# Where the last transposes of a SwiGLU's shares stand in the DMA queue, and where their first quarter is added

## The chip, the cores and the metric

The kernel runs on one core of a Trainium2 chip. The metric is the device time of one execution in microseconds (us), the median of several runs. Times inside the profile are us from the start of its span. The engines are named as the profile names them: PE (TensorE), DVE (VectorE), ACT (ScalarE), POOL (GpSimd) and SP (SyncE), whose queue here only issues DMAs.

## The reference

Two layers, on x of 512 tokens by 1024 features, in float32:

```
for l in range(2):
    x = x + 0.5 * swiglu(rms_norm(x, g1[l]), wg1[l], wu1[l], wd1[l])      # width 2816
    h = rms_norm(x, gm[l])
    z = h @ w_in[l]                                                       # 2304 columns
    attn = sliding_window_attention(q, k, v from z, sink)                 # 8 heads of 64, window 128
    conv = b_gate * causal_conv3(c_gate * h_conv)
    x = x + concat(attn, conv) @ w_out[l]
    x = x + 0.5 * swiglu(rms_norm(x, g2[l]), wg2[l], wu2[l], wd2[l])
return rms_norm(x, final)

swiglu(h, wg, wu, wd) = (silu(h @ wg) * (h @ wu)) @ wd
```

## The kernel before

x is kept with features on the partitions: eight tiles `xs[c]` of 128 features by 512 tokens, two to an `xpair`. Each product is made of three float32r matmuls, high by high, low by high and high by low. So each weight tile that has been loaded (`raw`) is split: ACT casts it to `wh` (line 226), DVE subtracts that from it into `wl` (line 226 too), 128 x 1024 elements at a time. `order` is the list of weight tiles in the order of use; `take_split` hands out the next one and splits those up to two further on (`SPLIT_AHEAD`); `need_split` in turn calls `need_raw`, which puts the loads of tiles up to four further on (`LOAD_AHEAD`) into SP's queue, at that place of the program. There are 8 `raw` buffers and 3 each for `wh` and `wl`.

A SwiGLU is a list of stages. The three inner ones (first and second of layer 0, first of layer 1) have the list `INNER`: a plain stage "p" and its down projection "d" with one block; five "w" stages (two blocks of the width each, by a scheme of seven products); two groups of shares "s", which are the down projections of four blocks each, by seven products; and a last "d", the down projection of blocks 9 and 10.

The shares make their result the other way round, with tokens on the partitions, in `Apart`. It is kept as four quarters (o, t): o is the half of the features, t the half of the tokens. Three go back to x through the DMA: `Apart.send` has ACT lay the 16-bit halves of the words apart (`lay_apart`, line 141, two copies a quarter) and SP issue two DMA transposes (line 898); `Apart.back` has ACT join the halves (line 911, two copies of 128 x 1024 a quarter) and DVE add them to x (line 915, two additions). The fourth, (0, 1), goes through PE (eight transposes, line 921) and two additions by DVE (line 926). In the second group of shares `SENT_AT` sends (0, 0) after step 3, (1, 1) after step 4 and (1, 0) after step 5; after step 6, the last, `between` calls `back(1, 1)`.

Then comes the last "d". It has four weight tiles, d0 to d3, each for two of the eight feature tiles, and makes them in the order c = 4, 5, 6, 7, 0, 1, 2, 3, twelve matmuls each. After each, DVE adds the result to `xs[c]` (line 1250). After c = 4 `BACK_AT` calls `back(0, 0)` and `back(0, 1)`, after c = 5 `back(1, 0)`. The next norm's `take` (ACT line 458 makes `xh`, DVE line 459 makes `xl`) and `square` (ACT line 467, DVE line 468) follow for each c as `FINAL_AT` says. The next stage's first matmuls take `xh` and `xl` in the same order of c, and after its first group and two more steps PE needs the sum of squares (line 523).

The weights of the next stage are loaded by the same rule of four ahead. It puts two loads into SP's queue before the transposes of (1, 1), and two more before those of (1, 0). ACT, DVE and SP each run their instructions in the order in which they are queued.

This passage, the end of the second group of shares and the last "d", occurs three times. Its places are called here J1 (first SwiGLU of layer 0, PE starts the "d" at 313.55 us), J2 (second SwiGLU of layer 0, at 796.12) and J3 (first SwiGLU of layer 1, at 1118.50). After J1 and J3 comes the mixing with its weights `w_in`, after J2 the next SwiGLU with `wg` and `wu`.

Of the kernel before, what the change touches and what calls it, by code (L numbers as in the profile page):

```python
# [49 lines left out]


SENT_AT = {3: (0, 0), 4: (1, 1), 5: (1, 0)}
BACK_AT = {4: ((0, 0), (0, 1)), 5: ((1, 0),)}
FINAL_AT = {4: (), 5: (4, 5)}
STREAM_BACK_AT = {9: 0, 11: 1, 16: 2, 18: 3}
SCORES_AT = (5, 6, 7, 8, 9, 10, 12, 13)
# [10 lines left out]
LOAD_AHEAD = 4  # L67
# [8 lines left out]
def trunk_kernel(  # L76
# [23 lines left out]
    nc = tc.nc  # L100
# [92 lines left out]
    units = []  # L193
    order = []
    raw_of, split_of = {}, {}
    roomy = set()
    state = {"raw": 0, "split": 0, "group": 0, "late": None}

    def add_unit(*unit):
        units.append(unit)  # L200
# [10 lines left out]
    def need_raw(u):  # L211

        while state["raw"] <= min(u, len(units) - 1):
            n = state["raw"]
            _, _, kc, _, wide = units[n][0]
            name, shape = f"raw_{n}", (P, kc, wide)
            r = form(name, F32, shape) if n in roomy else stock(name, shape=shape)
            if n >= OPEN:
                load(r, n, 0, kc)
            for more in units[n][1:]:  # L220
                nc.gpsimd.dma_start(out=r, in_=rows_of(*more), accum_op=ALU.add)  # L221
            raw_of[n] = r
            state["raw"] += 1
# [10 lines left out]
    def need_split(g):  # L234
        while state["split"] <= min(g, len(order) - 1):
            n = state["split"]
            u, what = order[n]
            far = what == "far"
            if what in (None, "far"):
                need_raw(u if far else u + LOAD_AHEAD)  # L240
                raw = raw_of.pop(u)
            elif isinstance(what, tuple) and what[0] == "end":

                _, what, h = what
                at = {"a11": 2, "s2": 2, "s3": 3, "s1": 3, "a12": 4, "a22": 5, "s4": 5}[what]
                need_raw(u + 3 * at + h + LOAD_AHEAD)
                raws = {name: u + 3 * i + h for i, name in enumerate(END_LOADS)}
                if what == "s2":
                    with tc.issue_after(state["rest"]):
                        nc.vector.tensor_add(raw_of[raws["a11"]], raw_of[raws["a11"]], raw_of[raws["s1"]])  # L250
                raw = raw_of[raws["a11" if what in ("s2", "s4") else what]]
            elif isinstance(what, tuple):

                what, h, how = what
                far = how == "far"
                last = {"a11": 0, "a12": 4, "s2": 2, "s3": 6, "s1": 2, "a22": 8, "s4": 4}[what]
                need_raw(u + h if far else u + max(last, 4) + h + LOAD_AHEAD)
                a11, s1, a12, s3, a22 = (raw_of.get(u + 2 * i + h) for i in range(5))
                if what == "s2":

                    late = state["late"] if h else None
                    if not state["late"] and how == "share":
                        late = state["rest"]
                    with tc.issue_after(late) if late else nullcontext():
                        nc.vector.tensor_add(a11, a11, s1)  # L265
                raw = {"a11": a11, "a12": a12, "s2": a11, "s3": s3, "s1": s1, "a22": a22, "s4": a12}[what]
            shape = list(raw.shape)
            hi = wpool.tile(shape, F32R, tag="wh", bufs=3, name=f"wh_{n}")
            lo = wpool.tile(shape, F32R, tag="wl", bufs=3, name=f"wl_{n}")
            if far:  # L270
                sent = split_far(hi, lo, raw)
            else:
                state["cast"], state["rest"] = (i.ins for i in split(hi, lo, raw))
            if isinstance(order[n][1], tuple) and order[n][1][0] == "end":
                if what == "a12":
                    nc.gpsimd.dma_start(out=raw_of[raws["a11"]], in_=raw, accum_op=ALU.add)
                if what in ("s3", "s1", "a12", "a22"):
                    del raw_of[raws[what]]
                if what == "s4":
                    del raw_of[raws["a11"]]  # L280
            elif isinstance(order[n][1], tuple):
                if what == "s3" and how == "share":
                    nc.gpsimd.dma_start(out=a12, in_=a11, accum_op=ALU.add)
                elif what == "s3":
                    nc.vector.tensor_add(a12, a12, a11)
                done = {"s3": (0, 3), "s1": (1,), "a22": (4,), "s4": (2,)}.get(what, ())
                for i in done:
                    del raw_of[u + 2 * i + h]
            split_of[n] = (hi, lo)
            state["split"] += 1  # L290
            if far:

                with tc.issue_after(sent.ins):
                    need_raw(u + LOAD_AHEAD + (4 + h if isinstance(order[n][1], tuple) else 0))
# [63 lines left out]
    def plan():  # L358
# [19 lines left out]
        def ffn(wg, wu, wd, stages, near=False):  # L378
            for what, b in stages:
                how = "far" if b == (0,) and not near else None  # L380
                if what == "p":
                    plain(wg, wu, b)
                if what == "w":
                    seven(
                        lambda o, j, h: ((wg, wu)[o], KC // 2 * j + 2 * h, 2, 2 * b * P, S),
                        lambda what, h: "far" if (b, what, h) == (1, "a11", 0) else None,
                    )
                if what == "s":
                    seven(
                        lambda o, j, h: (wd, 2 * b + KC // 2 * j + 2 * h, 2, o * S, S),  # L390
                        lambda what, h: "share",
                    )
                if what == "d":
                    cols(wd, 2 * b[0], 2 * len(b), KC, how, len(b) == 2)
                if what == "e":
                    u = len(units)
                    roomy.update(range(u, u + 3))
                    for form_ in END_LOADS:
                        ojs = {"s1": ((1, 0), (1, 1)), "s3": ((1, 0), (0, 0))}
                        for i in range(3):  # L400
                            add_unit(
                                *(
                                    (wd, 2 * b + (KC + 2 * j if i == 2 else KC // 2 * j + 2 * i), 2, o * S, S)
                                    for o, j in ojs.get(form_, ((0, int(form_ == "a12")) if form_ != "a22" else (1, 1),))
                                )
                            )
                    order.extend((u, ("end", what, i)) for what in END_FORMS for i in range(3))
# [470 lines left out]
    class Apart:  # L878
# [14 lines left out]
        def send(self, o, t):  # L893

            to = self.sent[o, t] = g8(f"turned_{self.name}_{o}_{t}", U16, (P, 2, NT, H))
            for u in range(2):
                halves = lay_apart(self.y[2 * t + u, o], f"{self.name}_{o}_{2 * t + u}")
                nc.sync.dma_start_transpose(
                    to.rearrange("p a c s -> p (a c) s")[:, :, u * P : (u + 1) * P],
                    halves.rearrange("p a n -> p (a n)"),  # L900
                )

        def back(self, o, t):

# [27 lines left out]
    def ffn(norm, stages, after=None, late=None):  # L932
# [248 lines left out]
        for i, (what, b) in enumerate(stages):  # L1181
# [22 lines left out]
            elif what == "e":  # L1204
                end.last(ends, kept)
                return
            elif what == "s" and b == sevens[0]:
                then = shared(sevens[1])
                share(
                    ops,  # L1210
                    0.5,
                    joined(ahead(then, {3: ("b11",), 4: ("b21",), 5: ("t2",), 6: ("t3",)})),
                    apart,
                    still=kept,
                )
            elif what == "s":

                def between(step):
                    if step == 1:
                        crossing[0].rejoin(1)  # L1220
                    if step in (4, 5):
                        with tc.issue_after(state["rest"]):
                            crossing[0].parts(step - 4)
                    if step in SENT_AT:
                        apart.send(*SENT_AT[step])
                    if step == 6:
                        apart.back(1, 1)

                share(then, 0.5, between, apart, behind=(1, 2, 3), on=kept)
# [10 lines left out]
            for c, acc in down(rhs, b == (0,), final):  # L1240
# [11 lines left out]
                    )  # L1252
                flush()
                if final:
                    for quarter in BACK_AT.get(c, ()):
                        apart.back(*quarter)
                    for k in FINAL_AT.get(c, (c,)):
# [478 lines left out]
```

## Time and profile before

| | us |
|---|---|
| median of 3 runs (lowest, highest) | 1630.61 (1630.34, 1632.09) |
| the profiled execution's own time | 1632.9 |
| its span, first to last instruction | 1631.1 |
| PE busy | 1616.7 |
| DVE busy | 1368.8 |
| ACT busy | 1178.1 |
| POOL busy | 223.6 |

The granted TensorE clock was 0.999 of full speed. Rows of a timeline give the start, the length, the engine, the line, the operation, what it writes and reads, how many such instructions the row merges, and in square brackets the time for which the engine stood idle before it and what ended that. A row of waits gives who waited for whom, the sum in us, the number of times and the longest. Matmul ends are modelled: a 128 x 512 matmul is shown as 0.39 long, and when nothing holds PE up the next one starts 0.227 after it.

### The profile page before, as it was taken

The numbers are of one execution on the slowest core, as the hardware profiler recorded it, in microseconds if no ns is written. First come the engines' busy times: TensorE is split into PE (matmuls) and PEld (weight loads), VectorE is DVE, ScalarE is ACT, GpSimd is POOL, SyncE is SP. The second block draws the span as 40 slices with busy tenths as digits, with TensorE's granted clock in tenths as the row PEclk, the third lists the DMA queues.
The fourth block names the chain that finished last, engine by engine and source line by source line (L and its number), as shares of the span: only waits on it lengthen the run. The fifth ranks groups of instructions, "written<-read, shape, count | busy, mean of one in ns | idle before, by whom it ended". The sixth has DMA issues, their size and how long they took to land.

```text
span 1631.1 us, 21176 instructions
## 1 busy us (share of the span) xinstructions
PE 1616.7 (99%) x7572; PEld 1348.1 (83%) x7572; DVE 1368.8 (84%) x1779; ACT 1178.1 (72%) x1510; POOL 223.6 (14%) x199
## 2 busy tenths in 40 slices
PE   9999999999999999999999999999999999999998
PEld 6788888878898888888888888888788988888887
DVE  7978797888899977797999777989788998677997
ACT  6667777867766577778865777787586767878665
POOL 1211111001121111111011111110012111111121
PEclk9999999999999999999999999999999999999999
DMA  9899989922597698999967999999135978999992
GB/s 271 198 237 212 210 210 239 242 68 73 129 238 180 178 217 213 214 213 247 228 143 188 217 215 219 214 237 221 52 91 152 233 152 215 225 220 231 240 250 71
DMA packets 307166, 318.12 MB, mean 195 GB/s; under 512 B 125612, under 2 KB 188660, under 8 KB 307060
## 3 DMA queue, kind: packets, MB, share of 16 engines
q1 hardware_dynamic: 265140, 230.63, 49.9%
q0 software_dynamic: 41200, 85.47, 30.5%
q8 instruction: 59, 0.97, 0.2%
q10 hardware_dynamic: 720, 0.66, 0.1%
q14 instruction: 47, 0.39, 0.1%
HBM read 264.29 MB, written 2.10 MB: 163 GB/s over the span
## 4 chain that ended last, share of the span: by engine, by line
PE 91%; DVE 5%; ACT 2%; DMA 1%; issue 1%; SPq 0%; ACTq 0%; DVEq 0%
PE x L824 26%; PE y L824 13%; PE x_s L824 9%; PE w L824 6%; PE acc L313 6%; PE acc L312 6%; PE acc L315 6%; PE y_s L824 5%; PE w_s L824 3%; PE x_m L809 3%; PE y_m L809 1%; DVE wl L226 1%; PE y_e L824 1%; PE acc L686 1%; PE x_e L824 1%
## 5 line engine op out<-in xcount | busy, mean ns | idle before, releaser
L226 DVE TENSOR_TENSOR wl<-raw,wh 128x1024 fp32r<-128x1024 f32 (+1 forms) x493 | 599.6, 1224 | 171.8 <-ACT wh L226 171.0
L226 ACT CAST wh<-raw 128x1024 fp32r<-128x1024 f32 (+1 forms) x493 | 513.9, 1046 | 302.2 <-PE x L824 95.0
L313 PE MATMUL acc<-xl,wh 128*128 128x512 f32 x392 | 153.6, 392 | 2.8 <-DVE xl L459 2.8
L312 PE MATMUL acc<-xh,wh 128*128 128x512 f32 x392 | 153.4, 393 | 0.5 <-ACT wh L226 0.5
L315 PE MATMUL acc<-xh,wl 128*128 128x512 f32 x384 | 149.6, 390 | 0.0
L221 POOL DMA_DIRECT2D raw<-in_ffn_wu_dram x40 | 50.2, 1264 | 386.1 <-DVE wl L226 203.8
L313 PEld LDWEIGHTS acc<-xl,wh 128*128 128x128 f32 x392 | 73.7, 188 | 18.7 <-DVE xl L459 4.4
L312 PEld LDWEIGHTS acc<-xh,wh 128*128 128x128 f32 x392 | 73.7, 188 | 15.5 <-ACT wh L226 0.6
L315 PEld LDWEIGHTS acc<-xh,wl 128*128 128x128 f32 x384 | 72.1, 188 | 15.0
L221 POOL DMA_DIRECT2D raw<-in_ffn_wg_dram x40 | 49.4, 1261 | 200.9 <-DMA raw<-in_ffn_wu_dram 82.9
L221 POOL DMA_DIRECT2D raw<-in_ffn_wd_dram x34 | 41.0, 1206 | 246.3 <-DMA raw<-in_ffn_wd_dram 109.7
L265 DVE TENSOR_TENSOR raw<-raw,raw 128x1024 f32<-128x1024 f32 x58 | 70.6, 1221 | 3.6 <-DMA raw<-in_ffn_wu_dram 3.2
L1086 ACT COPY raw_a<-turned 128x1024 uint16<-128x1024 uint16 x48 | 63.5, 1357 | 0.0
L824 PE MATMUL x<-wl,ft2h 128*128 128x512 f32 x160 | 62.2, 390 | 1.1 <-DVE wl L226 1.1
L824 PE MATMUL y<-wh,ft4h 128*128 128x512 f32 x160 | 62.4, 390 | 0.1
L824 PE MATMUL w<-wh,fb21h 128*128 128x512 f32 x160 | 62.3, 390 | 0.0
L824 PE MATMUL y<-wh,ft3h 128*128 128x512 f32 x160 | 62.3, 390 | 0.0
L824 PE MATMUL w<-wl,fb21h 128*128 128x512 f32 x160 | 62.3, 389 | 0.0
L824 PE MATMUL x<-wh,ft2h 128*128 128x512 f32 x160 | 62.3, 389 | 0.0
L824 PE MATMUL x<-wh,ft1h 128*128 128x512 f32 x160 | 62.3, 389 | 0.0
L824 PE MATMUL x<-wh,ft2l 128*128 128x512 f32 x160 | 62.3, 389 | 0.0
L824 PE MATMUL x<-wh,ft1l 128*128 128x512 f32 x160 | 62.3, 389 | 0.0
(506 smaller groups left out, 4545.2 us busy)
## 6 DMA issues: line engine op xcount, KB each, us to landing
raw<-in_ffn_wu_dram SPq DMA_DIRECT2D x127, 512.0 KB, 5.4
raw<-in_ffn_wd_dram SPq DMA_DIRECT2D x105, 512.0 KB, 5.8
raw<-in_ffn_wg_dram SPq DMA_DIRECT2D x86, 512.0 KB, 5.3
raw<-in_ffn_wu_dram POOLq DMA_DIRECT2D x40, 512.0 KB, 8.9
raw<-in_ffn_wg_dram POOLq DMA_DIRECT2D x40, 512.0 KB, 6.2
raw<-in_w_in_dram SPq DMA_DIRECT2D x36, 512.0 KB, 4.0
raw<-in_ffn_wd_dram POOLq DMA_DIRECT2D x34, 512.0 KB, 9.4
raw<-raw POOLq DMA_DIRECT2D x21, 512.0 KB, 7.9
```

Source lines behind the costliest of these rows:

```text
L221: nc.gpsimd.dma_start(out=r, in_=rows_of(*more), accum_op=ALU.add)
L226: return nc.scalar.copy(hi, raw), eng.tensor_sub(lo, raw, f32(hi))
L265: nc.vector.tensor_add(a11, a11, s1)
L312: nc.tensor.matmul(acc, hi[:, k, :], rhs[k][0], start=k == first, stop=False)
L313: nc.tensor.matmul(acc, hi[:, k, :], rhs[k][1], start=False, stop=False)
L315: nc.tensor.matmul(acc, lo[:, k, :], rhs[k][0], start=False, stop=k == last)
L686: nc.tensor.matmul(opening[n], (lo if part == "w" else hi)[:, k, :], xl if part == "x" else xh, start=n not in begun, stop=k == KC - 1 and ...
L809: nc.tensor.matmul(accs[c // 2][:, c % 2, :], w[:, k, cols], x_[:, 2 * h + k, :], start=start and c % 2 == 0 and h + k + i == 0, stop=h + ...
L824: nc.tensor.matmul(accs[u], x_[:, 2 * h + k, tok], w[:, k, :], start=start and h + k + i == 0, stop=h + k == 2 and i == 2, skip_group_chec ...
L1086: nc.scalar.copy(words(raws[self.b][:, c, :]), self.to[:, :, c, :])
```

## The change

In the three inner SwiGLUs the loads of the next stage's weights are held back: from step 0 of the second group of shares (`hold`) `need_raw` goes no further than the last tile of the closing "d", and from c = 5 on the loads are put behind the last DMA transpose (`behind`, `apart.last`). In SP's queue the order "2 loads, transposes (1, 1), 2 loads, transposes (1, 0)" becomes "transposes (1, 1), transposes (1, 0), 4 loads". And `back(0, 0)` moves from after c = 4 to before `back(1, 1)`: on ACT its two copies now stand before those of (1, 1) and before the cast of d2, which stood between; on DVE its two additions stand before those of (1, 1). The numbers of instructions of each engine stay the same, and the order on PE and on POOL does too.

```diff
-BACK_AT = {4: ((0, 0), (0, 1)), 5: ((1, 0),)}
+BACK_AT = {4: ((0, 1),), 5: ((1, 0),)}
...
-    state = {"raw": 0, "split": 0, "group": 0, "late": None}
+    state = {"raw": 0, "split": 0, "group": 0, "late": None, "hold": None, "behind": None}
+    closing = []
...
             if n >= OPEN:
-                load(r, n, 0, kc)
+                with tc.issue_after(state["behind"]) if state["behind"] else nullcontext():
+                    load(r, n, 0, kc)
...
             if what in (None, "far"):
-                need_raw(u if far else u + LOAD_AHEAD)
+                need_raw(u if far else max(u, min(u + LOAD_AHEAD, state["hold"] or len(units))))
...
                 if what == "d":
                     cols(wd, 2 * b[0], 2 * len(b), KC, how, len(b) == 2)
+                    if len(b) == 2:
+                        closing.append(len(units) - 1)
...
-                nc.sync.dma_start_transpose(
+                self.last = nc.sync.dma_start_transpose(
                     to.rearrange("p a c s -> p (a c) s")[:, :, u * P : (u + 1) * P],
                     halves.rearrange("p a n -> p (a n)"),
-                )
+                ).ins
...
+                    if step == 0:
+                        state["hold"] = closing[norm.i // 3 * 2 + norm.i % 3 // 2]
                     if step == 6:
+                        apart.back(0, 0)
                         apart.back(1, 1)
...
                 if final:
+                    if c == 5:
+                        state["hold"], state["behind"] = None, apart.last
+                    if c == 0:
+                        state["behind"] = None
                     for quarter in BACK_AT.get(c, ()):
                         apart.back(*quarter)
```

## The prediction

> **What bounds the kernel now.** I read the page's busy times first, then PE's waits, then the timelines of PE, DVE, ACT and SP around the three places J1, J2 and J3.
>
> ```profile
> span 1631.1 us, 21176 instructions
> PE 1616.7 (99%) x7572; PEld 1348.1 (83%) x7572; DVE 1368.8 (84%) x1779; ACT 1178.1 (72%) x1510; POOL 223.6 (14%) x199
> ...
> PE acc L313 <- DVE xl L459: 2.8, 4, 1.1
> ```
>
> PE is busy for all but 14 us of the span, and the change takes no matmul away, so all it can win is time in which PE stands still. The largest entry of PE's own waits is matmuls of line 313 that waited for `xl`, four times. They stand in the first group behind the closing "d". Here are that "d"'s first matmul, the one that waited longest and the first matmul of the squares at J1; the same three at J2, where nothing waited; the first and the last at J3:
>
> ```profile
> 313.55 0.39 PE L312 MATMUL acc<-ah,wh 128*128 128x512 f32 x1
> 341.75 0.50 PE L313 MATMUL acc<-xl,wh 128*128 128x512 f32 x1 [1.05 <-DVE xl L459]
> 344.96 0.39 PE L523 MATMUL ssq<-sqh,ones_r 128*128 128x512 f32 x1
> ...
> 796.12 0.39 PE L312 MATMUL acc<-ah,wh 128*128 128x512 f32 x1
> 823.76 0.39 PE L313 MATMUL acc<-xl,wh 128*128 128x512 f32 x1
> 825.57 0.39 PE L523 MATMUL ssq<-sqh,ones_r 128*128 128x512 f32 x1
> ...
> 1118.50 0.39 PE L312 MATMUL acc<-ah,wh 128*128 128x512 f32 x1
> 1150.21 0.40 PE L523 MATMUL ssq<-sqh,ones_r 128*128 128x512 f32 x1
> ```
>
> PE does the same matmuls in the three. They take 344.96 - 313.55 = 31.41 at J1, 825.57 - 796.12 = 29.45 at J2 and 1150.21 - 1118.50 = 31.71 at J3. J2 has no stall, so J1 loses 1.96 and J3 2.26 against it: **4.22 us together, the most there is to win.** (The waits' 2.8 is less, because a matmul's shown length covers part of each stall.)
>
> Why `xl` is late shows on DVE and ACT, J1 first:
>
> ```profile
> 313.84 1.28 DVE L891 SCALAR_TENSOR_TENSOR apart<-x_s,apart 128x512 f32<-128x512 f32 x2
> 317.55 0.69 DVE L915 TENSOR_TENSOR x<-x,back 128x512 f32<-128x512 f32 x1 [2.43 <-ACT back L911]
> 319.68 1.23 DVE L226 TENSOR_TENSOR wl<-raw,wh 128x1024 fp32r<-128x1024 f32 x1 [0.21 <-ACT wh L226]
> 321.42 1.42 DVE L915 TENSOR_TENSOR x<-x,back 128x512 f32<-128x512 f32 x2
> 322.76 1.27 DVE L926 TENSOR_TENSOR x<-x,back 128x512 f32<-128x512 f32 x2
> 325.83 1.22 DVE L226 TENSOR_TENSOR wl<-raw,wh 128x1024 fp32r<-128x1024 f32 x1
> ...
> 799.32 1.23 DVE L226 TENSOR_TENSOR wl<-raw,wh 128x1024 fp32r<-128x1024 f32 x1 [0.21 <-ACT wh L226]
> 805.48 1.22 DVE L226 TENSOR_TENSOR wl<-raw,wh 128x1024 fp32r<-128x1024 f32 x1
> 822.24 0.75 DVE L459 SCALAR_TENSOR_TENSOR xl<-x,par,xh 128x512 fp32r<-128x512 f32 x1
> ```
>
> ```profile
> 311.62 1.05 ACT L226 CAST wh<-raw 128x1024 fp32r<-128x1024 f32 x1
> 316.17 2.57 ACT L911 COPY back<-turned 128x1024 uint16<-128x1024 uint16 x2 [3.50 <-DMA turned<-halves]
> 318.60 1.04 ACT L226 CAST wh<-raw 128x1024 fp32r<-128x1024 f32 x1
> 319.54 5.04 ACT L911 COPY back<-turned 128x1024 uint16<-128x1024 uint16 x4
> 324.44 1.05 ACT L226 CAST wh<-raw 128x1024 fp32r<-128x1024 f32 x1
> ...
> 794.19 1.04 ACT L226 CAST wh<-raw 128x1024 fp32r<-128x1024 f32 x1
> 795.79 2.59 ACT L911 COPY back<-turned 128x1024 uint16<-128x1024 uint16 x2 [0.56 <-DMA turned<-halves]
> ```
>
> At J1 ACT stands for 3.50 until the transposes of quarter (1, 1) land, DVE stands for 2.43 behind it, and from then on DVE has no hole in which to catch up. At J2 the same quarter lands 0.56 after ACT is free. The last `wl` of the "d" (d3's) is a good mark of how late DVE is: it starts 325.83 - 313.55 = 12.28 after PE's start of the "d" at J1, and 805.48 - 796.12 = 9.36 at J2. At J2 the last `xl` is ready at 822.24 + 0.75 = 822.99 and used at 823.76: **a slack of 0.77** at a mark of 9.36.
>
> SP's queue and ACT's copies into halves at J1, the step of the chain in which (1, 1) lands, and the longest pair of transposes (J3):
>
> ```profile
> 304.45 1.07 SPq L209 DMA_DIRECT2D raw<-in_ffn_wd_dram  x2
> 305.63 1.74 SPq L209 DMA_DIRECT2D raw<-in_w_in_dram  x2
> 307.45 6.53 SPq L898 DMA_TRANSPOSE turned<-halves  x2
> 314.07 1.16 SPq L209 DMA_DIRECT2D raw<-in_w_in_dram  x2
> 315.32 4.51 SPq L898 DMA_TRANSPOSE turned<-halves  x2
> ...
> 304.87 2.00 ACT L141 COPY halves<-apart 128x1024 uint16<-128x1024 uint16 x2 [0.15 <-DVE apart L891]
> 309.72 2.00 ACT L141 COPY halves<-apart 128x1024 uint16<-128x1024 uint16 x2
> ...
> 311.66 4.43 DMA turned<-halves
> ...
> 1101.62 8.12 SPq L898 DMA_TRANSPOSE turned<-halves  x2
> ```
>
> The first of (1, 1)'s halves is ready about 305.9, but SP is at the two `w_in` loads until 307.37, and the transposes are issued from 307.45 to 313.98 and land at 311.66 + 4.43 = 316.09, 2.1 after the pair's issue ends.
>
> **The change part by part.**
>
> *The loads leave the front of the transposes.* SP can issue (1, 1) from 305.9. I let the pair take the 6.53 that it took behind the loads: issue ends at 312.4, and it lands at 314.5. It should be quicker without them, but no row shows this pair without loads ahead of it; the bounds are the shortest pair, 4.51, which lands at 312.5, and the longest, 8.12, at 316.1. I take 6.53, the same pair's own row. (1, 0) has its halves at 311.72 and follows at once: with 4.51 its issue ends near 317.0, and it lands near 319.1.
>
> *Quarter (0, 0) goes into ACT's hole.* It had been sent a step earlier. After the cast of d1 (at 311.62; the next instruction starts some 0.95 behind a cast, as at 318.60 and 319.54, so ACT is free at 312.57) ACT now has four copies in a row, (0, 0) then (1, 1), then the cast of d2. Four copies cost 324.44 - 319.54 = 4.90. The copies of (1, 1) start at 312.57 + 2.45 = 315.02, behind the 314.5 of their landing, so they do not wait. The cast of d2 starts at 317.47 and d2's `wl` 1.08 later (319.68 - 318.60), at 318.55. From d2's `wl` to d3's DVE took 805.48 - 799.32 = 6.16 at J2 without a hole; without the two additions of (0, 0), which cost 322.76 - 321.42 = 1.34 and now run before, it is 4.82. So the mark comes at 323.37, 9.82 after PE's start: 2.46 earlier than before at J1, 0.46 later than now at J2, within the slack of 0.77. (1, 0), landed near 319.1, is copied by 321.7 and d3 cast by 322.7, in time for 323.37.
>
> The two edits thus work together. J2 and J3 have the same order on each engine: at J2 ACT is free at 794.19 + 0.95 = 795.14, so (1, 1) is wanted at 797.6 and has landed by 795.79 even now. **J1 wins its 1.96, J3 its 2.26, J2 loses nothing: 4.22.** What is late next is `xl` still, but 0.77 - 0.46 = 0.31 on the safe side. I take off 0.1 for the jitter that so thin a margin lets through: 4.1.
>
> *The four loads go out later.* They are `w_in` at J1 and J3, `wg` and `wu` at J2. Nothing is queued behind a waiting instruction because of it except SP's own following loads, which wait for buffers anyway. Issued from about 317.1, two per 1.16, they are out by 319.5.
>
> ```profile
> 329.50 1.04 ACT L226 CAST wh<-raw 128x1024 fp32r<-128x1024 f32 x1
> ...
> DMA to landing us min/median/max: 3.6/4.0/7.3
> ...
> DMA packets 307166, 318.12 MB, mean 195 GB/s; under 512 B 125612, under 2 KB 188660, under 8 KB 307060
> ```
>
> The first cast of a `w_in` tile is that at 329.50, now about 327.0 with the earlier chain. Loads of `w_in` land 3.6 to 7.3 after issue (second row, the view of that tensor's instructions), here by 324.5 at the worst for the first; the others are wanted one by one after it. So this edit costs nothing, and what hides it is the 10 us of the "d" still to run.
>
> The Trainium skill's page "DMA: Bandwidth & Descriptors" (Rules for kernel authors) speaks against it: issue a DMA early, compute, and wait for it late. By that rule the loads give up some 11 us of lead, and the sum would be the second rival's. The trace does not bear the rule out here, as far as the row of landings goes.
>
> POOL's order is unchanged, and PE's too, so nothing else is priced. From the profiled execution's own 1632.9 the sum gives 1628.8. That execution is 2.3 over the median of the runs, 0.8 over the highest. I subtract the same 4.1 from the median: **1626.5 us.** If the whole 2.3 were stalls at these places that other executions don't have, only 1.9 would be left to win, 1628.7; I can't see it in one trace, and keep it for the range.
>
> **The rivals.** About 0.2% (3.3 us) is what a measurement of this kernel can tell from no change.
>
> *First: the transposes are slow by themselves.* If (1, 1) takes the longest pair's 8.12, it lands at 316.1, 1.1 after ACT wants it; with 0.31 of slack that stalls each of the three places by 0.8, J2 too. 4.22 - 2.4 = 1.8 is left: 1628.8. For it: that pair stands in the rows. Against: at this place it took 6.53, and two loads that stood right ahead of it are gone.
>
> *Second: the weights come late.* Seven loads now leave in one burst (the four and the three that follow). If they shared the bandwidth, the first would land with the last: 7 x 0.524 MB at 195 GB/s are 18.8 us, at 335.9. The cast and the subtraction (1.05 and 1.22) end at 338.1. At J2 the group of the first such tile starts 30 matmuls of 0.227 before the squares, 22.6 after the "d"; so at J1 it starts at 336.2, and its third matmul wants the `wl` at 336.7. Three times 1.4 eats the gain: 1630.6, no change. Against it: the 3.6 to 7.3 of the row. This is what the Trainium skill's rule just named would make of the change.
>
> *Third, slower: ACT waits longer than now.* ACT's queue behind the copies of (1, 1) holds the cast of d2, the copies of (1, 0) and the cast of d3, so a late landing holds up all of them and DVE with them, now at J2 as well. It decides the sign when (1, 1) lands more than 0.31 + 4.22 / 3 = 1.7 after ACT wants it, at 316.7 in J1's time, later than now. The slowest landing of these transposes is 9.2 us after issue:
>
> ```profile
> DMA to landing us min/median/max: 3.3/4.6/9.2
> ```
>
> Were the second of (1, 1), issued 311.66 - 307.45 = 4.2 after the first and so at 310.1, to take that, it would land at 319.3: 4.3 late, 4.0 lost at three places, 12.0 - 4.2 = 7.8 slower, 1638.4. Against it: fewer loads are ahead of it than now.
>
> That the change does not do what it says is excluded by the order of the changed program's instructions: the four loads stand behind the last transpose in all three places.
>
> **How the numbers follow.** The forecast, stalls gone or nearly, 0.68: 1625.8 to 1627.3. First rival and the smaller stalls of other executions, 0.17: 1627.3 to 1629.5. Second, 0.05: 1630.6. Third, 0.10. The first two make the range, 1625.5 to 1629.5, with 0.85. Faster by over 0.2% is the forecast, 0.68; within 0.2% the first two rivals, 0.22; slower 0.10.
>
> **What would show it.** In the profile after: no wait of line 313's matmuls for `xl` at J1 and J3, and 29.5 from the "d"'s first matmul to the squares at all three; ACT's four copies in a row from 312.6, with no wait for a DMA between them; d3's `wl` 9.8 after PE's start. It is wrong if ACT still waits for transposes, if J2 shows a new wait for `xl`, or if casts of `w_in` wait for a DMA.

## The result, and the profile after

The changed kernel took **1629.55 us** (median of 22 runs, 1628.29 to 1632.10), the kernel before beside it 1632.87 (22 runs, 1629.60 to 1638.06): a ratio of 0.9978, 95% interval 0.9970 to 0.9985. In a second set it was 1628.80 against 1629.98, a ratio of 0.9991 (0.9982 to 1.0000). So it is faster by 0.1 to 0.2% in both. That is little against the scatter: the kernel before, run unaltered once more in the second set, came out at 1.0012 (1.0000 to 1.0023) of its own other runs. So the argument rests on the stages in the profiles and on the longest times more than on one median. The direction is the forecast's. The 4.1 us (0.25%) lies inside the first interval, near its lower end, and outside the second, and no run of either kernel came below 1627.42, so the 1626.5 was lower than any execution seen.

The page of the profiled execution (1631.99 us), and two of PE's waits that the kernel before did not have:

```profile
span 1630.2 us, 21175 instructions
PE 1618.0 (99%) x7572; PEld 1349.4 (83%) x7572; DVE 1368.1 (84%) x1779; ACT 1178.0 (72%) x1510; POOL 223.7 (14%) x199
...
PE x_s L828 <- DVE wl L228: 1.0, 1, 1.0
PE y_s L828 <- DVE wl L228: 0.7, 2, 0.5
```

The matmuls that waited for `xl` are gone, and waits in the shares have come. First the three places. The closing "d"'s first matmul and the first matmul of the squares at J1, J2 and J3, from PE's timeline:

```profile
313.31 0.39 PE L314 MATMUL acc<-ah,wh 128*128 128x512 f32 x1
342.76 0.39 PE L527 MATMUL ssq<-sqh,ones_r 128*128 128x512 f32 x1
...
794.10 0.39 PE L314 MATMUL acc<-ah,wh 128*128 128x512 f32 x1
823.55 0.39 PE L527 MATMUL ssq<-sqh,ones_r 128*128 128x512 f32 x1
...
1119.84 0.39 PE L314 MATMUL acc<-ah,wh 128*128 128x512 f32 x1
1149.30 0.39 PE L527 MATMUL ssq<-sqh,ones_r 128*128 128x512 f32 x1
```

They are 29.45, 29.45 and 29.46 apart, where 31.41, 29.45 and 31.71 stood. SP's queue, ACT and DVE at J1, from their timelines:

```profile
302.78 1.07 SPq L210 DMA_DIRECT2D raw<-in_ffn_wd_dram  x2
305.71 7.43 SPq L902 DMA_TRANSPOSE turned<-halves  x4
313.23 7.39 SPq L210 DMA_DIRECT2D raw<-in_w_in_dram  x6
```

```profile
311.38 1.05 ACT L228 CAST wh<-raw 128x1024 fp32r<-128x1024 f32 x1
312.33 5.00 ACT L915 COPY back<-turned 128x1024 uint16<-128x1024 uint16 x4
317.18 1.06 ACT L228 CAST wh<-raw 128x1024 fp32r<-128x1024 f32 x1
318.12 2.60 ACT L915 COPY back<-turned 128x1024 uint16<-128x1024 uint16 x2
320.55 1.08 ACT L228 CAST wh<-raw 128x1024 fp32r<-128x1024 f32 x1
```

```profile
318.27 1.23 DVE L228 TENSOR_TENSOR wl<-raw,wh 128x1024 fp32r<-128x1024 f32 x1 [0.21 <-ACT wh L228]
...
323.01 1.22 DVE L228 TENSOR_TENSOR wl<-raw,wh 128x1024 fp32r<-128x1024 f32 x1
```

SP issues the four transposes in one run of 7.43, from the moment that the halves are there. ACT makes four copies in a row with no wait for a DMA (in the first profile of before its copies waited four times for transposes, 7.7 in all; in this one never), and d3's `wl` starts 323.01 - 313.31 = 9.70 after the "d" (9.69 and 9.78 at J2 and J3).

Yet this span is only 0.9 shorter than the first one of before. From J1's "d" to J3's it takes 1119.84 - 313.31 = 806.53, before 1118.50 - 313.55 = 804.95 with 1.96 of stall in it: 3.54 were lost elsewhere, most of it in the shares ahead of J3. There DVE's `wl` came late:

```profile
1069.01 0.50 PE L828 MATMUL y_s<-wl,ft4h_s 128*128 128x512 f32 x1 [0.53 <-DVE wl L228]
...
1103.79 0.50 PE L828 MATMUL x_s<-wl,ft1h_s 128*128 128x512 f32 x1 [1.01 <-DVE wl L228]
```

POOL's two accumulations `raw<-raw` in that stretch, for which SP's `wd` loads wait, landed 9.5 and 13.6 after issue (5.7 and 9.0 at the same place in the first profile of before). In the second profile of the same kernel (1628.83 us) these stalls are not there, and the three stages are 29.45 again; it has one other stall, ahead of J2:

```profile
571.80 0.50 PE L828 MATMUL w<-wl,fb21h 128*128 128x512 f32 x1 [1.05 <-DVE wl L228]
```

So the change does not cause the stalls ahead of J3 in every execution. Whether it makes them more likely is open: of the five profiles of kernels with both edits, three wait for `wl` at the matmul of the last row (1.01 here, 0.90 and 1.23 below), and of the nine other profiles none does.

### The profile page after: what moved, and what is told of

Its sections match the earlier page's. It is cut to its first block, busy times and chain, and to the rows that moved or that the text cites. A ratio compares the mean times of both kernels' runs of the same rounds, so it can differ in the third digit from the quotient of the medians.

```text
span 1630.2 us, 21175 instructions
## 1 busy us (share of the span) xinstructions
PE 1618.0 (99%) x7572; PEld 1349.4 (83%) x7572; DVE 1368.1 (84%) x1779; ACT 1178.0 (72%) x1510; POOL 223.7 (14%) x199
## 4 chain that ended last, share of the span: by engine, by line
PE 91%; DVE 3%; DMA 3%; ACT 2%; issue 1%; SPq 0%; ACTq 0%; DVEq 0%; POOLq 0%
PE x L828 26%; PE y L828 13%; PE x_s L828 8%; PE acc L314 7%; PE acc L315 7%; PE acc L317 7%; PE w L828 6%; PE y_s L828 4%; PE x_m L813 3%; PE w_s L828 2%; DMA raw<-in_ffn_wd_dram 2%; PE y_m L813 1%; DVE wl L228 1%; PE y_e L828 1%; PE x_e L828 1%; PE acc L690 1%
## 5 line engine op out<-in xcount | busy, mean ns | idle before, releaser
L828 PE MATMUL x<-wl,fb11h 128*128 128x512 f32 x160 | 62.3, 389 | 0.0
```

Source lines behind the costliest of these rows:

```text
L828: nc.tensor.matmul(accs[u], x_[:, 2 * h + k, tok], w[:, k, :], start=start and h + k + i == 0, stop=h + k == 2 and i == 2, skip_group_chec ...
```

## The experiments

They ran in three sets of four, each with runs of the kernel before on the same chip: 1629.98 (35 runs), 1631.28 (35) and 1630.15 (29). Everything "of the d" is counted from PE's start of that closing "d".

**The loads alone.** The changed kernel with quarter (0, 0) joined where it was:

```diff
-BACK_AT = {4: ((0, 1),), 5: ((1, 0),)}
+BACK_AT = {4: ((0, 0), (0, 1)), 5: ((1, 0),)}
...
                     if step == 6:
-                        apart.back(0, 0)
                         apart.back(1, 1)
```

> Only the loads are moved behind the last transposes; the first quarter is joined after c = 4 as before. Theory A (the transposes are slow because loads stand ahead of them in SP's queue): each transpose of (1, 1) is issued in 1.2 to 1.7 us instead of 2.3 to 4.3 and lands before ACT has cast d1, ACT's wait for it is gone, the last wl of the closing d starts some 9.3 us after PE's start of the d (12.28 before at J1), and the stage from the d's first matmul to the squares is 29.45 at J1, J2 and J3; time as the changed kernel, 0.998 of before. Theory B (what helped is that the first quarter's additions leave DVE's busy stretch, and the place of the loads does little): the stage stays 31 or more at J1 and J3, time within 0.1% of before.

Measured: 1628.73 (1628.07 to 1630.60), ratio 0.9987 (0.9975 to 0.9998), all three stages 29.45, and d3's `wl` at 8.64, 8.74 and 8.60. PE, SP and DVE at J1, and PE at J3:

```profile
313.36 0.39 PE L314 MATMUL acc<-ah,wh 128*128 128x512 f32 x1
342.81 0.39 PE L527 MATMUL ssq<-sqh,ones_r 128*128 128x512 f32 x1
...
305.75 7.42 SPq L902 DMA_TRANSPOSE turned<-halves  x4
...
322.00 1.22 DVE L228 TENSOR_TENSOR wl<-raw,wh 128x1024 fp32r<-128x1024 f32 x1
...
1116.12 0.39 PE L314 MATMUL acc<-ah,wh 128*128 128x512 f32 x1
1145.58 0.39 PE L527 MATMUL ssq<-sqh,ones_r 128*128 128x512 f32 x1
```

**The loads' move alone takes the stalls away**, and its time is that of both edits in the same set (1628.80). The quarter's move does not help here; it puts the mark 1.0 later (9.70).

**The quarter alone.** The kernel before with the opposite edit: `back(0, 0)` in front of `back(1, 1)`, the loads where they were.

> Only the first quarter is joined and added in the last step; the loads stay ahead of the transposes. Theory A: (1, 1) still lands near 316 at J1, ACT has joined (0, 0) by then, d2's wl stands where it stood and d3's comes 1.34 us earlier, 10.9 after PE's start of the d at J1; the stage is 30.3 at J1 and 30.5 at J3, 29.45 at J2; half or more of the gain, 0.9985 to 0.999 of before. Theory B: 29.45 at all three, time as the changed kernel.

Measured: 1629.38, ratio 1.0000 (0.9991 to 1.0008). J3 kept its stall, 1147.74 - 1116.34 = 31.40. ACT and SP there, from their timelines:

```profile
1115.36 2.58 ACT L911 COPY back<-turned 128x1024 uint16<-128x1024 uint16 x2
1118.96 2.57 ACT L911 COPY back<-turned 128x1024 uint16<-128x1024 uint16 x2 [1.03 <-DMA turned<-halves]
1121.40 1.04 ACT L226 CAST wh<-raw 128x1024 fp32r<-128x1024 f32 x1
1124.81 2.56 ACT L911 COPY back<-turned 128x1024 uint16<-128x1024 uint16 x2 [2.37 <-DMA turned<-halves]
```

```profile
1109.17 1.61 SPq L209 DMA_DIRECT2D raw<-in_w_in_dram  x2
1110.90 5.75 SPq L898 DMA_TRANSPOSE turned<-halves  x2
1117.08 1.01 SPq L209 DMA_DIRECT2D raw<-in_w_in_dram  x2
1118.18 4.30 SPq L898 DMA_TRANSPOSE turned<-halves  x2
```

The hole ahead of (1, 1) shrank, and then ACT waited 2.37 for (1, 0), which is behind the second pair of loads: d3's `wl` stayed at 12.28. I had expected a stage of 30.5 here, and had overlooked that (1, 0) is next in line. At J1 the stage was 29.59.

**Both kernels again.** The kernel before and the changed one, unaltered.

> The kernel before, unchanged, for a second profile. If the stalls at J1 and J3 are steady: stages of 31.4 and 31.7 again. If they depend on when the transposes happen to land: other values between 29.45 and 33, J2's too, and the runs spread by several us as they did (1629.6 to 1638.1).

> The changed kernel, unchanged, for a second profile. Theory A: 29.45 at all three places again, whatever else differs. The stalls of some 3.4 us in the shares ahead of J3 (1067 to 1104 us in the first profile of this kernel) are there again if the change made them, gone or elsewhere if they are chance.

Before: 1631.26 (1628.20 to 1637.55). After: 1628.80 (1628.07 to 1630.32). The profile of before is the surprise. It is an execution of 1628.49 us, span 1626.7, and at J1 it shows no stall worth the name (PE, SP, ACT and DVE):

```profile
313.70 0.39 PE L312 MATMUL acc<-ah,wh 128*128 128x512 f32 x1
343.17 0.39 PE L523 MATMUL ssq<-sqh,ones_r 128*128 128x512 f32 x1
...
306.09 4.87 SPq L898 DMA_TRANSPOSE turned<-halves  x2
...
314.41 2.57 ACT L911 COPY back<-turned 128x1024 uint16<-128x1024 uint16 x2 [1.62 <-DMA turned<-halves]
...
324.04 1.22 DVE L226 TENSOR_TENSOR wl<-raw,wh 128x1024 fp32r<-128x1024 f32 x1
```

The stage is 29.47, with ACT's wait 1.62 in place of 3.50 and d3's `wl` at 10.34; J2 and J3 are at 29.45. **The 4.22 us of the first profile are not in every execution.**

**The kernel before a third time**, for its profile.

> The kernel before once more, for its profile alone. Theory: its time over the floor of 1628.2 is the sum of what its three stages have over 29.45 and of stalls in the shares; each stage's excess is the start of d3's wl less 10.3 (0 below), and that start goes with the landing of the second transpose of (1, 1): near 10.3 at 0.6, near 12.3 to 12.6 at 2.5. Rival: an execution over 1630 with all three stages at 29.45.

Measured: 1629.59 us, stages 30.29, 29.45 and 29.81. All profiles with the old order of loads lie on one line, stage = 29.45 + (start of d3's `wl` - 10.32), and at 29.45 where that start is earlier:

| kernel, place | d3's `wl` | stage over 29.45 |
|---|---|---|
| before, first profile, J1 / J3 | 12.28 / 12.58 | 1.96 / 2.26 |
| quarter alone, J1 / J3 | 10.46 / 12.28 | 0.14 / 1.95 |
| before, second profile, J1 | 10.34 | 0.02 |
| before, third profile, J1 / J3 | 11.16 / 10.68 | 0.84 / 0.36 |

The executions' times less these sums are 1632.9 - 4.22 = 1628.7, 1630.40 - 2.09 = 1628.3, 1628.49 - 0.02 = 1628.5 and 1629.59 - 1.20 = 1628.4: what these four differ by is these stalls, to within 0.4.

**Only the first pair of loads moved.** As "the loads alone", but SP's order is (1, 1), two loads, (1, 0), two loads:

```diff
+                    if step == 4:
+                        state["hold"], state["behind"] = None, apart.last
...
-                    if c == 5:
-                        state["hold"], state["behind"] = None, apart.last
```

> The changed kernel with quarter (0, 0) joined where it was before, and only the first two of the four loads moved: SP's order is (1, 1), two loads, (1, 0), two loads. Theory (only what stands ahead of (1, 1) counts, because ACT's queue behind its copies holds everything else): (1, 1) is issued at -7.6 of the d's start and takes under 2 for each transpose, as without loads; (1, 0) takes about 3 for its first behind the two loads and lands near 3 to 5.5, before ACT wants it near 6. d3's wl 8.6 to 9.5 after PE's start, 29.45 at all three, and a time within 0.1% of the kernel with all four moved (1628.7 against 1630.0 of before). Rival (both pairs count, as the run with only the quarter moved suggests, where (1, 0) was the late one): (1, 0) lands after 6.5, d3's wl over 10.3, and a stage of 29.6 to 30.5 at one place or more; time as before.

Measured: 1629.03, ratio 0.9986 (0.9976 to 0.9995); stages 29.45, d3's `wl` at 8.64, 8.64 and 8.95. SP at J1:

```profile
305.71 2.58 SPq L902 DMA_TRANSPOSE turned<-halves  x2
308.39 1.16 SPq L210 DMA_DIRECT2D raw<-in_w_in_dram  x2
310.55 4.65 SPq L902 DMA_TRANSPOSE turned<-halves  x2
```

Two pairs of transposes of one size, in one execution: **2.58 for the pair without loads right ahead, 4.65 for the pair behind two loads.** The second of these pairs, (1, 0), took 2.59 in the changed kernel, where no load stands ahead of it. It has room for that, if (1, 1) is on time. Only the pair of loads ahead of (1, 1) had to go.

**A delay on SP in both orders.** Three small copies on SP's queue, one ahead of (1, 1) and two ahead of (1, 0), each waiting until the one ahead of it has landed; in the kernel before the third one stands behind the second pair of loads:

```diff
+                    if step == 4:
+                        hold_queue(3, apart.y[2, 1][:, :P])
```

> The kernel before with three small copies on SP's queue, each of which waits until the one ahead has landed: one stands ahead of (1, 1), one ahead of the two loads and one ahead of (1, 0). By the 3.6 to 4 that a load takes to land, (1, 0) goes out some 3 to 4 later than before and the rest hardly later. Theory (a late landing is the stall, and the kernel before has next to no room for it): (1, 0) lands 7 to 11 after the d's start also where the queue is on time, d3's wl is at 11.5 to 14, and the stages are 30.5 to 33 at all three places: 4 to 8 slower than the kernel before, 1634 to 1638. Rival (the time is set elsewhere, and the stalls of the first profile went with another cause): stages move by less than 0.5, time within 0.1% of before.

> The changed kernel with the same three copies on SP's queue: one ahead of (1, 1) and two ahead of (1, 0), no load between. Theory: (1, 1) lands as in the changed kernel or 1 later, near -3 to -1; (1, 0) waits for one landing and lands at 3 to 5, when ACT wants it near 5; d3's wl at 9.7 to 10.2, 29.45 to 29.6 at all three places, time within 0.1% of the changed kernel: the changed order has some 4 of room for (1, 0) that the order before lacks. Rival (the change only moved the critical landing, and there is no room): a landing over 6, d3's wl over 10.5 and stages over 30 here too.

Before: stages 29.45, 29.45 and 30.37, and 1633.76 (1631.74 to 1641.76), ratio 1.0019 (1.0004 to 1.0035). The stages do not explain that time. The profiled execution, the fastest of the ten, lost 0.92 in them and reached J1 2 us late from the start of the program; what the others lost is not shown. After: 29.45 at all three, 1628.82 (1628.38 to 1631.33), ratio 0.9989 (0.9978 to 1.0000).

The copies delayed much less than I had meant. In the kernel before they landed 2.1 to 6.2 after issue, but most of that time passed while the transposes and loads between them were issued; (1, 0) went out at 0.43, -0.69 and 1.34 of the "d", against 1.77, -1.21 and 1.79 in the first profile of before and -0.53, -2.75 and -1.65 in the second. In the changed kernel they landed after about 2, and (1, 0) went out 0.3, 0.3 and 2.2 later than in its first profile. So the size of the effect on the old order was missed, and the room of the changed order is shown for a delay of 2 at one place, not for the 4 of my expectation.

**The weights still later.** Four such copies between the last transpose and the four loads of the changed kernel:

```diff
-                        state["hold"], state["behind"] = None, apart.last
+                        with tc.issue_after(apart.last):
+                            state["behind"] = hold_queue(4, apart.y[2, 0][:, :P])
+                        state["hold"] = None
```

> The changed kernel with four small copies, each waiting for the landing of the one ahead, between the last transpose and the four loads: the loads leave some three landings, 10 to 13, later, near 10 to 14 after the d's start in place of 0 to 2.5. Theory (the lead of the weights is dead time, about 10 more than wanted): the first cast of the next weights, wanted near 13.7, waits 2 to 6 for its load, but PE wants the tile only near 23, so the stages keep 29.45, no matmul of the first group waits over 0.5, and the time is within 0.1% of the changed kernel. Rival (the rule to issue loads early holds and the changed kernel already stands at the edge): matmuls of the first group wait 1 to 5 at each place for wh or wl, and the kernel is 3 to 12 slower.

SP and ACT's first cast of the next weights at J1, and a wait of PE ahead of J3:

```profile
314.49 5.99 SPq L172 DMA_DIRECT2D pad<-apart  x4
320.53 23.77 SPq L217 DMA_DIRECT2D raw<-in_w_in_dram  x12
...
326.86 1.04 ACT L235 CAST wh<-raw 128x1024 fp32r<-128x1024 f32 x1
...
1101.66 0.50 PE L835 MATMUL x_s<-wl,ft1h_s 128*128 128x512 f32 x1 [0.90 <-DVE wl L235]
```

The loads left 320.53 - 313.53 = 7.0 after the "d", 7 later than in the changed kernel but earlier than the 10 to 14 that I had expected, and the first cast, for which I had expected a wait of 2 to 6, still did not wait for a DMA. Stages 29.45 at all three. The time was 1630.32, ratio 0.9991 (0.9980 to 1.0002): 1.5 or 0.09% over the delayed kernel of the same set (1628.82), just inside my 0.1%. In its profile PE waited 0.90 for a `wl` in the share ahead of J3 (the last row) and some tenths in a later stage, neither for these loads. Whether the copies cause that is open.

**A later queue, from POOL.** One small copy on POOL's queue ahead of the first of the two `raw<-raw` accumulations of each share, in the kernel before, the changed one and "the loads alone":

```diff
                 if what == "s3" and how == "share":
+                    if not h:
+                        for _ in range(1):
+                            nc.gpsimd.dma_start(out=pad, in_=a11[:, 0, :P])
                     nc.gpsimd.dma_start(out=a12, in_=a11, accum_op=ALU.add)
```

> The kernel before with one small copy (128 x 128) on POOL's queue in each share, right ahead of the first of the two accumulations of one weight tile into another (raw<-raw). SP's four wd loads ahead of the transposes wait for that accumulation, so all of SP's queue should run 1 to 1.5 later in every execution. Theory (the stalls of the first profile come with a late queue: in that profile the accumulation landed at -21.2 and -20.9 of the d's start at J1 and J3 and the stages had 1.96 and 2.26 more; in the second profile at -22.1 and -22.3, with next to nothing): it lands near -20.5 to -21, (1, 1) lands at 1.5 to 2.5, d3's wl is at 11.5 to 12.6, and the stage is longer by that less 10.3: 1.2 to 2.3 at J1 and J3, 0 to 1 at J2. Time 2 to 4.5 over the floor of 1628.2 in nearly every execution: 1631 to 1634, no run under 1629.5. Rival (the stalls have another cause, and the late queue only goes along with it): stages as in the second profile, 29.45 to 29.5, and times as before, 1628 to 1634.

> The changed kernel with the same copy on POOL's queue. Theory: the four wd loads are as late as in the kernel before with that copy, but no load stands ahead of (1, 1): it is issued at -7 to -5, lands at -2.5 to 0.5, before ACT wants it near 1.4; d3's wl at 9.7 to 9.9, 29.45 at all three, time 1628.5 to 1630.0 (the shares may lose some tenths to the copy itself), 0.1 to 0.3% under the kernel before with the copy. Rival: (1, 1) lands after 2, d3's wl over 10.5, and stages over 29.6 at J1 or J3.

> The kernel with only the loads moved and the same copy on POOL's queue. Theory (the loads' move alone makes the order safe, and quarter (0, 0) ahead of d2's cast only puts d3's wl 1.0 later): landings as in the changed kernel with the copy, d3's wl 8.6 to 9.3, 29.45 at all three, time within 0.05% of the changed kernel with the copy. Rival (the quarter's move pays when the queue is late, because ACT then has work while (1, 1) is on its way): (1, 1) lands after 0, ACT waits for it, d3's wl over 10.3 and some tenths of stall at J1 or J3, time 0.05 to 0.15% over the changed kernel with the copy.

Measured: 1630.67 (ratio 1.0003, 0.9994 to 1.0013), 1631.02 (1.0005, 0.9995 to 1.0015) and 1630.08 (1.0004, 0.9993 to 1.0014). On time this is inconclusive, and against me: three runs of the first are under 1629.5, which I had excluded, and the other two kernels lost their gain. The stages did as expected in kind: 30.07, 29.64 and 29.45 in the first (d3's `wl` at 10.94, 10.51 and 9.38, on the line of the table), 29.45 six times in the others. But the copy did not make the queue late everywhere, as I had meant. SP's first `wd` load, which waits for the accumulation, went out 21.8 ahead of J2's "d" (23.6 to 24.2 in the three profiles of before), which gave J2 its first stall, 0.19; at J1 and J3 it went out 21.6 and 21.7 ahead, within the spread of before (20.6 to 22.2). And the shares now stall, in the changed kernel's profile by this:

```profile
1102.63 0.50 PE L833 MATMUL x_s<-wl,ft1h_s 128*128 128x512 f32 x1 [1.23 <-DVE wl L230]
```

So time is lost to late weights in a second place, outside the three stages. The first kernel's profile has a wait of 1.0 for another DMA (`ft4l_m`), also outside them. What makes SP's queue late at J1 and J3 in some executions stays open: the first `wd` load went out 21.1, 22.1 and 20.6 ahead of J1's "d" in the three profiles of before, and the stalls were 1.96, 0.02 and 0.84, which is not in order.

## Why the prediction was right, and where not

**The chain was right, step by step.** It put (1, 1)'s issue at 305.9, the four copies at 312.57, the cast of d2 at 317.47, d2's `wl` at 318.55 and d3's at 323.37, which is 9.82 after the "d". Measured: 305.71, 312.33, 317.18, 318.27 and 323.01, 9.70 after it, with the whole stage 0.24 earlier. The stages came to 29.45 at J1 and J3 and J2 lost nothing.

**The edge was nearly right.** From J2 I read that a mark over 9.36 + 0.77 = 10.13 stalls; the table has 10.32.

**The transposes were mis-sized, on the safe side.** I let (1, 1) take 6.53 without loads, for want of a row. It took 2.58 at J1, 3.38 at J2 and 4.93 at J3, where the two `wd` loads ahead of it were late. Its second transpose landed 2.3 ahead of the "d"'s start at J2 and 0.6 at J3 (at J1 the trace lacks that landing), 3.8 and 2.1 before ACT's copies of it, where I had 0.5. So "the two edits thus work together" fell: with the pair that quick, the loads' move is enough, and the quarter's move costs 1.0 of the mark's room. What it gives in return is time for (1, 1): at J1 ACT takes up its copies 1.46 after the "d"'s start with both edits and 0.99 ahead of it with the loads' move alone. No run with the loads moved needed that time.

**The step that failed is the last: "I subtract the same 4.1 from the median".** It took the profiled execution's 4.22 for every execution's. The kernel before, profiled twice more, had 0.02 and 1.20. The prediction had the right sentence, that the 2.3 by which that execution lay over the median might be stalls that others don't have, which leaves 1.9 and gives 1628.7, and kept it for the range instead of taking it as the forecast. Measured were 1628.80 and 1629.55, the second 0.05 above the stated range. That the first ratio, 0.9978, came near the forecast's is in part luck: the kernel before had a median of 1632.87 in that set, and 1629.98, 1631.28 and 1630.15 in the others. What the change takes away is mostly the long times: in the first set 12 of 22 runs of before were above 1632.10, of the changed kernel none; in all four sets together 39 of 121 runs of before, and none of the 56 of the changed kernel, "the loads alone" and "only the first pair". How much of those long times these stalls make up is not shown, as no execution above 1632.9 was profiled, and with the copy on POOL's queue 7 of 23 runs with the loads moved were above 1632.10 again. The lowest runs differ little: 1627.42 to 1629.60 before, by set, 1628.07 and 1628.29 after.

**The rivals.** The transposes are not slow by themselves (2.58 to 4.93, and none too late). ACT does not wait longer than now: no copy of (1, 1) waited. And the weights do not come late: no cast waited for them, nor with 7 us less of lead. The Trainium skill's "DMA: Bandwidth & Descriptors" (Rules for kernel authors), to issue a DMA early and wait for it late, would have had the loads stay in front. In these runs their lead was worth nothing, and what it cost stood behind them in the same queue: at J1 4.07 to 6.53 for the pair (1, 1) with two of them ahead and 2.58 to 2.74 without. At J3 it was 4.40 to 5.75 against 2.58 to 4.93, at J2 3.18 to 5.23 against 2.58 to 4.58, so there the ranges overlap.

## What to carry to other kernels

In a queue that works in order, look at what stands ahead of the transfer that something waits for next; a load that is wanted 10 us later goes behind it. A stall that one profile shows may be that execution's alone: before it is taken off the median, compare the execution's time with the spread of the runs, because a profile that lies above the median can hold stalls that other runs don't have. And read which transfer is late next: with only the quarter moved, the wait passed from (1, 1) to (1, 0) and the time stayed.

## What the runs showed of the hardware that I had not expected

- In one execution a pair of DMA transposes was issued in 2.58 with no load right ahead of it, and another pair of the same size in 4.65 behind two 512 KB loads.
- A 64 KB copy from one tile to another landed 1.8 to 2.2 us after issue where no load stood right ahead of it, so that four in a chain took 5.99 to issue; in the delayed kernel before, among loads, it landed after 2.1 to 6.2.
- An accumulating copy of one weight tile into another landed 4.7 to 11.6 after issue over all profiles, and 13.6 once, in an execution that then stalled in the shares.
